# One retention head ahead of the four HGRN2 heads, and the last two modulation chunks computed in the downward stage

## The chip, the core and the metric

The kernel runs on one core of a Trainium2 chip. A core has a matrix engine (PE, with its weight loads listed apart as PEld), a vector engine (DVE), a scalar engine (ACT), a general engine (POOL) and sixteen DMA engines that are fed from queues; the queue of SP carries most transfers here and the queue of ACT the rest. Each engine works through its own list of instructions in order and waits on semaphores for the others. The metric is the device time of one execution in microseconds (us).

## The reference

One transformer block for 2048 rows of width 1024 and a context of 256 rows, all in float32. What matters here:

```python
mod_x = (silu(c) @ w_mod + b_mod)            # sh1, sc1, g1, sh2, sc2, g2, 1024 columns each
hx = rmsnorm(x, norm1_g) * (1 + sc1) + sh1   # 2048 rows; hc the same for the 256 context rows
p  = h @ w_in                                # hq, hi, hff, hfb, hg (HGRN2) and rq, rk, rv, rg (retention)
# HGRN2, 4 heads of 128: f = lb + (1 - lb) * sigmoid(z), forward and backward, k = 1 - f
#   scan in both directions with a decay per channel; rmsnorm((o_f + o_b) * sigmoid(hg))
# retention, 4 heads of 128: rotary embedding of rq and rk (x only), a fixed decay per head,
#   scan in both directions; rmsnorm(y_f + y_b) * silu(rg)
# both scans start from states that the context gives
x = x + g1 * (concat(8 heads) @ w_out)
h2 = rmsnorm(x, norm2_g) * (1 + sc2) + sh2
gate, up = split(h2 @ w_up)                  # 2 x 2816 columns
x = x + g2 * ((silu(conv3(gate)) * up) @ w_down)
return rmsnorm(x, final_g)
```

## The kernel before, in words

Matrices are multiplied in float16 pairs: each float32 operand is split into a high and a low part, and each product is three matmuls (`mm3`, lines 88 to 90). On top of that the products run as Winograd's form of Strassen's scheme: seven block products instead of eight, with sums of blocks made by DVE, ACT and POOL beforehand (`first_blocks` for the rows, `pair_blocks` for the weights) and sums of results afterwards (`unit`).

**Startup** (`setup`, `mod_first`, `heads`). The silu of c and c_ctx is multiplied by the columns of `w_mod` in chunks of 512; a chunk is called j4, and twelve chunks make the six vectors. Chunks 2, 3, 0 and 1 (scale and shift of the first norm) are multiplied on PE at the start, and the loads for it stand in SP's queue among those of the rows and of the first head's weights (`head_weights`, its loads and its preparation are items that are worked off one by one). `lower_bounds` makes the HGRN2 lower bounds with an exponential.

**Rows.** The 2048 rows are four groups g of 512. `norm_rows` and `first_blocks` turn a group into the seven block operands `hx` in float16 pairs. This takes DVE (lines 378, 387, 413, 416, 431), ACT (412, 433) and POOL (413, 451). Groups 3, 2, 1, 0 are made while the first head runs: `with_blocks` takes a step of the head's projection and a step of the next group's blocks by turns. The blocks are also written to DRAM (`hxd`), from where every later head reads them.

**Heads.** Eight heads run one after the other, HGRN2 0 to 3 and then retention 0 to 3. A head takes four steps, groups 3, 2, 1, 0. In a step, the head's backward sweep of one group (`hg_sweep1` or `ret_sweep1`) runs together with the forward sweep of a group of the head before (`sweep2`, `sweep2b`) and, as a filler, with the projection of the next group (`hg_proj`, `ret_proj`); `weave` says how many steps of the filler go between those of the sweep. The HGRN2 sweep goes through seven levels of doubling blocks, each with products on DVE (lines 874, 879, 759) that feed the next; the retention sweep has one decay mask and no levels. The context states come in a head's first step.

Alongside, `tick` works off a list: the next head's weights, and during the retention heads 0, 1 and 2 the chunks 4 to 6, 7 to 9 and 10 to 11 of the modulation (`mod_later`), which are eight DVE instructions of 128x512 each (lines 301, 303) and a few small matmuls (`mod_rows`, line 244). `ret_consts` makes the decay tables of the retention heads (lines 1102 to 1131) at the first step of the third head. The second half of the kernel is the output projection, the upward stage with its convolution and the downward stage (`ffn_down`), where seven block products, each for two halves of the rows, run from 2280 us to the end and `finish` writes the output. The gate g2 is spread over partitions into `gb` (`broadcast_cols`, line 1288) after the first of these; the first products with `gb` (line 1736) run in the second one, from 2347.5 us on.

**What sets the order.** The program is written once in this order; a planner then simulates it with costs of its own and lays down the order of the instructions on each engine. Buffers are rings named by tags ("Kl" has three, "gate" five, "wr" two), and an instruction waits until its ring has a free place.

Of the kernel before, what the change touches and what calls it, by code (L numbers as in the profile page):

```python
# [18 lines left out]
P = 128  # L19
# [24 lines left out]
SEQUENCE = 0, 1, 5, 6, 4, 3, 2  # L44

# [9 lines left out]
class Kern:  # L55
# [77 lines left out]
    def setup(self):  # L133
# [42 lines left out]
        self.W0, self.items0 = self.head_weights(0)  # L176
# [22 lines left out]
        self.smalls = s2, s1  # L199

# [32 lines left out]
    def mod_rows(self, rows, nr, j4):  # L233
# [12 lines left out]
        bm = view(self.sv, V_BM + 4 * j4, [[1, 4], [0, nr]])  # L246
        nc.vector.tensor_tensor(o, ps[:, :, :nr], bm, ALU.add)

    def mod_loads(self):
# [4 lines left out]
        for j4, places in ((2, ("hx",) * 4), (3, ("hx",) * 4), (0, KEPT[:4]), (1, ("FG", "KTt", "ou0", "ou1"))):  # L254
# [8 lines left out]
            if j4 in (3, 1):  # L263
                self.items0[0 if j4 == 3 else 4][0]()
# [14 lines left out]
    def mod_later(self, j4):  # L279
# [5 lines left out]
        def item(k0):  # L285
            def load():

                st[k0] = w = [self.slot_tile([P, 512], F32, "q", "wm") for _ in range(2)]
                for kk in range(2):
                    nc.sync.dma_start(w[kk], wsrc[:, k0 + kk, 512 * j4:512 * j4 + 512])  # L290

            def comp():
                if k0 == 0:
                    st["acc"] = self.slot_tile([P, 512], F32, "FG", "macc")
# [9 lines left out]
                if k0 + 2 == KT:  # L304
                    self.mod_rows(acc, 1, j4)
# [227 lines left out]
    def unit(self, mm, shape, banks, temps, evac, lin=(None, None), first=False):  # L533
# [5 lines left out]
        if first:  # L539
# [28 lines left out]
            add(tb, tb, u, ALU.add)  # L568
# [123 lines left out]
    def head_weights(self, h):  # L692
# [11 lines left out]
        for nm, tag, cols in want:  # L704
            raws, st = [], {}

            def load(cols=cols, raws=raws, tag="ou2" if h == 0 and nm == "q" else "wr"):
# [4 lines left out]
            def start(nm=nm, tag=tag, raws=raws, st=st):  # L712
# [7 lines left out]
                s, neg, dq = self.scales(self.allsum(ssq), self.dqx[:, 0:1] if h else None, "dq" + nm)  # L720
# [23 lines left out]
    def decay_gates(self, FG, X, h, n, W, first=False):  # L744
# [6 lines left out]
        yield from self.head_unit(*self.fm(w, X, n // 2), evac, first=first)  # L751
# [59 lines left out]
    def hg_proj(self, pool, h, g, W, pr, cur, first=False):  # L811
# [3 lines left out]
        yield from self.decay_gates(FG, X, h, G, W, first)  # L815
# [20 lines left out]
        yield from self.head_unit(*self.tm(w, X, H), evac, (dq, None), first)  # L836
# [125 lines left out]
    def hg_sweep2b(self, pool, h, g, st):  # L962
# [4 lines left out]
        m = r["qf"] if h < NH - 1 else pool.tile([P, G], F32, tag="Kl", bufs=KL, name="m")  # L967
# [14 lines left out]
    def step(self, h, i, W, cur, prev, pr):  # L982
# [3 lines left out]
        slot = i if h % 2 == 0 else NG - 1 - i  # L986
        hg, hgp = h < NH, h - 1 < NH
        if h < 2 * NH:
            main = (self.hg_sweep1 if hg else self.ret_sweep1)(pool, h % NH, g, slot, pr, cur)
        else:  # L990
            main = iter(())
        if prev is not None:
# [879 lines left out]
```

## Time and profile before

| | |
|---|---|
| median of 3 runs | 2695.32 us (2693.99 to 2698.18) |
| the profiled execution: its own time | 2692.15 us |
| its span, first to last instruction | 2690.3 us |
| mean granted clock of PE | 0.974 |
| busy in the span | PE 2532.6 us, DVE 1852.9, ACT 1335.7, POOL 776.8 |

How to read it: the span is counted from the first instruction; a stretch "46:309" is from 46 to 309 us after it. A row of a stretch gives for each engine its busy time and in brackets its instructions, then the clock that PE was granted as a part of full speed, the share of the DMA engines' time and the rate. A row of a group of instructions gives the line, engine and operation, out<-in, the count, and after the bar the busy time and the mean of one in ns; after the second bar stands how long the engine stood idle just before them and for whom. The head borders, read off the copies of each step's result: the first head's four steps end at 191, 229, 264 and 309 us, the three other HGRN2 heads at 476, 637 and 803 us, and the retention heads' sweeps end their last groups at 908, 1030, 1134 and 1234 us.

### The profile page before, as it was taken

How to read it: one execution, taken by the hardware profiler on the slowest of the kernel's cores; microseconds unless marked ns; L12 is line 12 of the kernel's file. 1: busy time of each engine (PE TensorE's matmuls, PEld its weight loads, DVE VectorE, ACT ScalarE, POOL GpSimd, SP SyncE). 2: the span in 40 equal slices, each digit the busy share in tenths (PEclk: the TensorE clock that was granted, in tenths of full speed). 3: DMA queues.
4: the chain of work that ended last, by engine and by line, in shares of the span. 5: the costliest groups of instructions: out<-in, count | busy, mean ns of one | idle time of the engine just before them, and what ended most of it. 6: DMA issues, size and time to landing. Idle time of an engine off the chain costs nothing.

```text
span 2690.3 us, 56082 instructions
## 1 busy us (share of the span) xinstructions
PE 2532.6 (94%) x22763; PEld 1669.3 (62%) x22763; DVE 1852.9 (69%) x3559; ACT 1335.7 (50%) x2846; POOL 776.8 (29%) x865
## 2 busy tenths in 40 slices
PE   5689999999999999998999899999999999999998
PEld 2578888888889889896444344444444444444443
DVE  4988667776767686767465878888888887323553
ACT  4766456664554444445455556555555555311210
POOL 3633112121123232221334344443443342000102
PEclk7899999999999999999999999999999999999999
DMA  7324234243337675756521223333323325634552
GB/s 262 145 84 158 87 119 147 73 154 118 104 130 254 194 249 185 250 182 198 198 98 48 94 91 118 102 110 114 118 98 106 116 92 203 247 131 187 203 196 94
DMA packets 213620, 393.97 MB, mean 146 GB/s; under 512 B 15599, under 2 KB 97747, under 8 KB 208752
## 3 DMA queue, kind: packets, MB, share of 16 engines
q1 hardware_dynamic: 203808, 373.42, 40.1%
q10 hardware_dynamic: 9248, 16.79, 1.9%
q8 instruction: 178, 2.92, 0.4%
q14 instruction: 82, 0.67, 0.1%
q0 software_dynamic: 304, 0.17, 0.0%
HBM read 298.57 MB, written 91.75 MB: 145 GB/s over the span
## 4 chain that ended last, share of the span: by engine, by line
PE 69%; DVE 16%; issue 5%; ACT 4%; DMA 3%; POOL 3%; SPq 0%; DVEq 0%; ACTq 0%; POOLq 0%
PE pa L88 7%; PE pa L89 7%; PE pa L90 7%; PE pd L88 5%; PE pd L90 5%; PE pd L89 5%; PE pc L88 3%; PE pc L89 3%; PE pc L90 3%; PE pb L88 2%; PE pb L89 2%; PE pb L90 2%; PE opp L88 2%; PE opp L89 2%; PE opp L90 2%
## 5 line engine op out<-in xcount | busy, mean ns | idle before, releaser
L88 PE MATMUL pa<-feat,w 128*128 128x512 f16 x704 | 264.5, 380 | 8.9 <-ACT ta L575 6.1
L89 PE MATMUL pa<-feat,w 128*128 128x512 f16 x704 | 267.5, 380 | 0.0
L90 PE MATMUL pa<-feat,w 128*128 128x512 f16 x704 | 266.9, 380 | 0.0
L89 PE MATMUL pd<-wd,actl 128*128 128x512 f16 x616 | 233.3, 379 | 0.0
L90 PE MATMUL pd<-wd,actl 128*128 128x512 f16 x616 | 233.3, 379 | 0.0
L88 PE MATMUL pd<-wd,actl 128*128 128x512 f16 x616 | 232.6, 379 | 0.0
L89 PEld LDWEIGHTS <-w 128*128 128x128 f16 x1232 | 120.6, 98 | 151.4 <-issue 13.2
L90 PEld LDWEIGHTS <-w 128*128 128x128 f16 x1232 | 120.8, 98 | 146.0 <-issue 1.7
L88 PEld LDWEIGHTS <-w 128*128 128x128 f16 x1232 | 120.7, 98 | 142.3 <-issue 2.6
L89 PEld LDWEIGHTS <-hx 128*128 128x128 f16 x1824 | 183.3, 100 | 7.4 <-issue 5.1
L88 PEld LDWEIGHTS <-hx 128*128 128x128 f16 x1824 | 183.5, 101 | 2.1
L90 PEld LDWEIGHTS <-hx 128*128 128x128 f16 x1824 | 182.8, 100 | 1.5 <-issue 0.7
L1622 ACT ACTIVATE st<-act,modT 128x512 f16<-128x512 f32 x154 | 107.3, 717 | 109.8 <-DVE act L1612 63.1
L1623 DVE SCALAR_TENSOR_TENSOR st<-act,modT,st 128x512 f16<-128x512 f32 x154 | 141.3, 953 | 29.6 <-ACT st L1622 28.9
L88 PE MATMUL pa<-w_vg,hx 128*128 128x128 f16 x800 | 145.2, 222 | 0.2
L90 PE MATMUL pa<-w_vg,hx 128*128 128x128 f16 x800 | 145.0, 222 | 0.0
L89 PE MATMUL pa<-w_vg,hx 128*128 128x128 f16 x800 | 144.9, 222 | 0.0
L88 PE MATMUL pc<-feat,w 128*128 128x512 f16 x352 | 134.0, 381 | 2.1 <-ACT feat L1397 1.1
L89 PE MATMUL pc<-feat,w 128*128 128x512 f16 x352 | 134.4, 382 | 0.1
L90 PE MATMUL pc<-feat,w 128*128 128x512 f16 x352 | 134.3, 382 | 0.0
L88 PE MATMUL pa<-hx,w_z 128*128 128x256 f16 x464 | 127.2, 274 | 5.5 <-DVE rV L617 4.1
L89 PEld LDWEIGHTS <-w_z 128*128 128x128 f16 x1072 | 107.3, 100 | 34.2 <-issue 23.7
(550 smaller groups left out, 7547.0 us busy)
## 6 DMA issues: line engine op xcount, KB each, us to landing
hx<-hxd SPq DMA_DIRECT2D x212, 512.0 KB, 4.6
actd<-st SPq DMA_DIRECT2D x154, 256.0 KB, 2.0
actl<-actd SPq DMA_DIRECT2D x28, 1024.0 KB, 5.0
wur<-in_w_up_dram SPq DMA_DIRECT2D x44, 512.0 KB, 3.8
raw<-in_w_in_dram SPq DMA_DIRECT2D x36, 512.0 KB, 4.4
wm<-in_w_mod_dram SPq DMA_DIRECT2D x64, 256.0 KB, 3.9
hxd<-hx SPq DMA_DIRECT2D x28, 512.0 KB, 3.6
wdb<-in_w_down_dram SPq DMA_DIRECT2D x44, 256.0 KB, 3.9
```

The source lines that it names most:

```text
L88: mm(ps, lhs(0), rhs(0), start=start, stop=False, skip_group_check=True)
L89: mm(ps, lhs(0), rhs(1), start=False, stop=False, skip_group_check=True)
L90: mm(ps, lhs(1), rhs(0), start=False, stop=stop, skip_group_check=True)
L1622: nc.scalar.activation(p[:, 0], v, AF.Copy, scale=s)
L1623: nc.vector.scalar_tensor_tensor(p[:, 1], v, s, p[:, 0], ALU.mult, ALU.subtract)
```

## The change

The heads run in the order retention 0, HGRN2 0 to 3, retention 1 to 3. So the rows' blocks are made beside a retention head. The tables of `ret_consts` are made in the startup, from loads on ACT's queue (`ret_loads`); `lower_bounds` moves into the first head's second step; the first head's weights are z and vg alone, without q; its rope tables come on SP's queue. Some temporaries lie in other buffers, and `with_blocks` spreads the blocks over 14 steps of the projection instead of 18. Chunks 10 and 11 of the modulation are taken out of retention head 2 and computed in the first three of the seven block products of the downward stage (`gates_later`), with `gb` behind them; the silu of c is kept in a place that lives that long (`keep`), and so is that part of the bias. Chunks 4 to 6 now go beside retention head 1 and 7 to 9 beside retention head 2. The output of a head goes through a tile of its own when the head behind is a retention head (`own`), and through `qf` otherwise.

```diff
+ORDER = 4, 0, 1, 2, 3, 5, 6, 7
...
-        self.W0, self.items0 = self.head_weights(0)
+        self.ret_loads()
+        self.W0, self.items0 = self.head_weights(ORDER[0], True)
...
         self.smalls = s2, s1
+        self.ret_consts()
...
     def mod_loads(self):
-            if j4 in (3, 1):
-                self.items0[0 if j4 == 3 else 4][0]()
+            if j4 == 3:
+                self.items0[0][0]()
...
-    def mod_later(self, j4):
+    def mod_later(self, j4, places=("q", "FG"), kept=False):
...
     def with_blocks(self, proj, blocks):
-        for j in range(18):
+        for j in range(14):
             next(proj)
-            if j in (5, 6, 7, 8, 9) or j > 11:
+            if 0 < j < 6 or j > 7:
                 next(blocks, None)
...
     def heads(self):
         self.mod_first()
-        items[5][0]()
         place = [self.gate_tile() for _ in range(4)]
         xc = self.load_rows(None, place)
         self.norm_rows(NG - 1, self.x3)
         for _, comp in items[:4]:
             comp()
-        self.lower_bounds()
+        items[4][0]()
...
-        first = self.hg_proj(pool, 0, NG - 1, W, pr, cur, True)
+        first = self.ret_proj(pool, ORDER[0] % NH, NG - 1, W, pr, cur, True)
...
-                    if NH <= h < 2 * NH - 1:
-                        mods = [it for c in ((4, 5, 6), (7, 8, 9), (10, 11))[h - NH] for it in self.mod_later(c)]
+                    if ORDER[p] in (5, 6):
+                        mods = [it for c in ((4, 5, 6), (7, 8, 9))[ORDER[p] - 5] for it in self.mod_later(c)]
...
-                blocks = self.first_blocks(0, rows(0, zq), self.temps(("ou2", "ou3", ("qf2", "qf3"), ("gate", "gate"))), "pj")
-            if s == 4 * 2:
-                self.ret_consts()
+                blocks = self.first_blocks(0, rows(0, zq), self.temps(("ou2", "ou3", "FG", ("gate", "gate"))), "pj")
+                self.lower_bounds()
...
+        keep = self.sv[:, V_LB + 6:V_LB + 14]
+        nc.vector.tensor_copy(keep, self.silc)
+        self.silc = keep
...
     def ret_proj(self, pool, h, g, W, pr, cur, first=False):
-            nc.scalar.dma_start(r, self.I["rope"][:, i, g * G:(g + 1) * G])
+            (nc.sync if first else nc.scalar).dma_start(r, self.I["rope"][:, i, g * G:(g + 1) * G])
...
+    def gates_later(self):
+        for j4 in (10, 11):
+            ahead = None
+            for load, comp in self.mod_later(j4, ("wr", "ou0"), True):
+                load()
+                yield
+                if ahead:
+                    ahead()
+                    yield
+                ahead = comp
+            ahead()
+            yield
+        dg = self.slot_tile([P, 2, P], F32, "xs", "diag")
+        self.broadcast_cols(lambda j: dg[:, j % 2], self.gb, 40)
+        yield
...
     def ffn_down(self):
+        late = self.gates_later()
...
                 self.work(1)
+                if n < 3:
+                    next(late, None)
             if m == 0 and t == 0:
-                dg = self.slot_tile([P, 2, P], F32, "xs", "diag")
-                self.broadcast_cols(lambda j: dg[:, j % 2], gb, 40)
                 fg = I["final_g"]
```

More of the change, by code (lines that the diff above doesn't have):

```diff
@@ L286, in load @@
             def load():
-                st[k0] = w = [self.slot_tile([P, 512], F32, "q", "wm") for _ in range(2)]
+                if places[0] == "wr":
+                    wr = self.slot_tile([P, 2, 512], F32, "wr", "wm")
+                    st[k0] = w = [wr[:, i] for i in range(2)]
+                else:
+                    st[k0] = w = [self.slot_tile([P, 512], F32, places[0], "wm") for _ in range(2)]
                 for kk in range(2):
@@ L705, in head_weights, with load @@
             raws, st = [], {}
-            def load(cols=cols, raws=raws, tag="ou2" if h == 0 and nm == "q" else "wr"):
+            def load(cols=cols, raws=raws, tag="wr"):
                 for c in cols:
@@ L814, in hg_proj @@
         FG = self.slot_tile([P, 2, G], F32, "FG", "FG")
-        yield from self.decay_gates(FG, X, h, G, W, first)
+        yield from self.decay_gates(FG, X, h, G, W)
         qs = pool.tile([P, G], F32, tag="qs", bufs=1, name="qs")
@@ L835, in evac @@
                 self.scaled(V[:, cs], c, s, dq)
[L836 removed]
+        yield from self.head_unit(*self.tm(w, X, H), evac, (dq, None))
         pr.update(FG=FG, K=K, Q=Q, qs=qs, ks=ks, V=V, gate=gate)
@@ L980, in weave, with step @@
             pass
-    def step(self, h, i, W, cur, prev, pr):
+    def step(self, p, i, W, cur, prev, pr):
         pool = self.mp
         g = NG - 1 - i
-        slot = i if h % 2 == 0 else NG - 1 - i
-        hg, hgp = h < NH, h - 1 < NH
-        if h < 2 * NH:
+        slot = i if p % 2 == 0 else NG - 1 - i
+        last = p == 2 * NH
+        h = None if last else ORDER[p]
+        hg = not last and h < NH
+        hp = ORDER[p - 1]
+        hgp = hp < NH
+        if not last:
             main = (self.hg_sweep1 if hg else self.ret_sweep1)(pool, h % NH, g, slot, pr, cur)
@@ L996, in step @@
             yield
-            if i == 0 and j == (1 if hg else 0) and h < 2 * NH:
+            if i == 0 and j == (1 if hg else 0) and not last:
                 yield from (self.hg_context if hg else self.ret_context)(pool, h % NH, W, cur)
-        if h or i:
+        if p or i:
             self.tick(self.n_tick)
         if prev is not None:
-            (self.hg_sweep2b if hgp else self.ret_sweep2b)(pool, (h - 1) % NH, i, prev)
+            sweep2b(pool, hp % NH, i, prev, not hg)
         yield from main
-        if h or i:
+        if p or i:
             self.tick(self.n_tick)
@@ L1212, in vg @@
                     self.scaled(V[:, cs], c, s, dqv)
-            yield from self.head_unit(*self.tm(w, X, H), vg, (dqv, None))
+            yield from self.head_unit(*self.tm(w, X, H), vg, (dqv, None), first)
             self.silu_bound(h, g, gate)
```

88 lines of the change are left out of this document (47 added, 41 removed).

## The prediction

> **What bounds the kernel now.** I read the page first, then busy time by stretches, then the chain of waits in the stretch that stands out.
>
> ```profile
> span 2690.3 us, 56082 instructions
> PE 2532.6 (94%) x22763; PEld 1669.3 (62%) x22763; DVE 1852.9 (69%) x3559; ACT 1335.7 (50%) x2846; POOL 776.8 (29%) x865
> ...
> DVE  4988667776767686767465878888888887323553
> PEclk7899999999999999999999999999999999999999
> PE 69%; DVE 16%; issue 5%; ACT 4%; DMA 3%; POOL 3%; SPq 0%; DVEq 0%; ACTq 0%; POOLq 0%
> ```
>
> PE is busy for 94% and carries 69% of the chain that ended last, so only PE's idle time, 158 us in all, and its slow clock can be won. Both sit at the left end: there DVE has its 9 and 8s and PEclk its only digits under 9. The stretches show how much lies there; the first head ends at 309 us, the HGRN2 heads at 803.
>
> ```profile
> core 0: us, PE busy (x) PEld busy (x) DVE busy (x) ACT busy (x) POOL busy (x), PEclk, DMA share, GB/s
> 46.00:85.00 39.00, 22.21 (x133) 16.26 (x133) 36.51 (x57) 28.03 (x55) 25.34 (x22) 0.63 0.42 155
> 104.00:229.00 125.00, 96.40 (x1404) 85.37 (x1403) 111.67 (x223) 84.79 (x201) 59.10 (x60) 0.88 0.28 107
> 46.00:229.00 183.00, 135.36 (x1770) 116.99 (x1771) 167.18 (x306) 128.22 (x287) 97.82 (x95) 0.84 0.34 125
> 46.00:309.00 263.00, 210.06 (x2960) 183.10 (x2961) 224.67 (x426) 172.24 (x382) 113.91 (x105) 0.87 0.37 129
> 309.00:803.00 494.00, 464.45 (x7640) 419.18 (x7638) 349.48 (x798) 273.00 (x685) 89.90 (x108) 0.98 0.35 117
> 816.00:936.00 120.00, 114.00 (x1382) 108.17 (x1382) 83.69 (x153) 55.85 (x142) 36.10 (x36) 0.99 0.67 221
> 1056.00:1166.00 110.00, 105.66 (x1255) 100.30 (x1254) 78.04 (x152) 48.68 (x126) 27.96 (x32) 0.98 0.65 218
> 816.00:1166.00 350.00, 332.31 (x3996) 315.42 (x3996) 245.79 (x460) 158.95 (x402) 98.94 (x104) 0.99 0.66 220
> 2275.00:2690.00 415.00, 406.08 (x1890) 185.24 (x1889) 175.61 (x265) 82.29 (x158) 34.19 (x116) 1.00 0.49 182
> ```
>
> From 46 to 229 us DVE is busy for 167.18 of 183 us (91%) and PE for 74%: here the rows are split into blocks beside the first head, and DVE sets the pace. From 309 to 803 us (three HGRN2 heads) PE is busy for 94%, from 816 to 1166 (three retention heads) for 95%: PE sets the pace, whatever the head. The chain of waits from 46 to 309 us, by line, says the same:
>
> ```profile
> by line: DVE ftmp L416 8.0%; DVE hx L413 7.3%; issue 5.1%; DVE Q L879 3.6%; PE p L88 3.3%; PE pa L88 3.1%; PE pa L89 3.1%; DVE ftmp L431 3.0%; PE p L89 2.9%; PE p L90 2.9%; PE pa L90 2.9%; DVE Q L822 2.8%; DVE junk L378 2.3%; DVE K L874 2.3
> ```
>
> Its largest pieces are DVE's block sums (416, 413), and the HGRN2 head's own products (879, 822, 874) stand in it with 8.7% of 263 us, 23 us.
>
> **The change part by part.** *The first head.* What the exchange takes off each engine comes from the two steady stretches, twelve steps each. DVE: 349.48/12 = 29.1 us in an HGRN2 step. A retention step has 245.79 us less the modulation chunks:
>
> ```profile
> L303 DVE SCALAR_TENSOR_TENSOR macc<-wm,silc,macc 128x512 f32<-128x512 f32 x56 | 47.4, 846 | 6.5 <-DMA wm<-in_w_mod_dram 5.9
> L1200 DVE TENSOR_TENSOR Q<-K,sin 64x1024 f32<-64x1024 f32 x12 | 18.8, 1566 | 9.4 <-ACT K L615 9.2
> L1222 DVE TENSOR_TENSOR K<-K,cos 128x1024 f32<-128x1024 f32 x13 | 17.7, 1365 | 0.0
> L301 DVE TENSOR_SCALAR macc<-wm,silc 128x512 f32<-128x512 f32 x8 | 4.6, 573 | 0.0
> ```
>
> (245.79 - 47.4 - 4.6)/12 = 16.1 us. The rotary products (1200, 1222 and its like) are in that. So 13.0 us per step go, 52 us over the head. PE: 464.45/12 - 332.31/12 = 38.7 - 27.7 = 11.0 per step, 44 us in all. What is left between 46 and 309 us is 172.7 us of DVE and 166 us of PE.
>
> How long does that take? At DVE's present share (224.67/263 = 85%) it is 202 us, 61 less; at PE's present share (80%) it is 208, 55 less. I take 60. By stretches: about 7 before 104 us, where q's weights and the gates' products go, 35 from 104 to 229, 18 after that, where PE leads. The bounds: at best DVE works at the 91% that it has up to 229 us, 172.7/0.91 = 190, 73 less; at worst only the HGRN2 pieces of the chain itself (23 us) and two thirds of the 18 go, 35 less.
>
> *Where the HGRN2 head lands.* It now costs what a steady one costs, 494/3 = 165 us. Out goes one of the three retention heads of 816 to 1166. Two stay: one as from 816 to 936 (120 us, twelve pairs of chunk instructions beside a head's weights) and one as from 1056 to 1166 (110 us), which now has 24 chunk instructions instead of 16. Eight more of 0.85 us make DVE 84.8 of 110 us, still under PE's 105.66; I charge half, 3.4. So 350 - 120 - 113.4 = 116.6 go and 165 come: **+48**. Bounds: 161 to 167 for the one (the three heads end at 476, 637 and 803 us), 110 to 120 for the other, so +41 to +57. The sweep of an HGRN2 group beside the forward sweep of a retention head has no row; its PE and DVE work is that of both, and POOL, through which the forward sweep's norm passes, is busy for 18% there.
>
> *The retention tables* leave the third head. Its first step stands beside the same step of the fourth:
>
> ```profile
> 476.00:529.00 53.00, 49.72 (x778) 45.11 (x776) 35.89 (x103) 28.71 (x71) 3.82 (x7) 1.00 0.23 76
> 637.00:690.00 53.00, 53.00 (x821) 48.63 (x820) 33.20 (x98) 24.70 (x64) 3.29 (x7) 1.00 0.22 77
> ```
>
> PE idles 3.3 us in the one and not at all in the other: **-3** (0 to -4). In the startup ACT has this hole for them:
>
> ```profile
> 15.64 0.63 ACT L376 ACTIVATE junk<-hc 128x512 f16<-128x512 f32 x1 [10.68 <-DMA hc<-in_x_dram]
> ...
> L1104 ACT ACT_TABLE_LOAD x1 | 1.3, 1283 | 0.0
> L1127 ACT ACTIVATE re<-ramp,tmp 128x128 f32<-128x128 f32 x8 | 2.8, 389 | 0.0
> ```
>
> Three table loads of 1.3 us, the eight exponentials of line 1127 and sixteen small ones come to about 11 us against 10.68 idle. The first squares (376) are next behind them on ACT, then the norm and the transposes, and PE's modulation matmuls queue behind those. I charge **+2** (0 to +6, half of the whole if the hole is missed). The ramp's load adds 256 KB to that time, and q's 512 KB go.
>
> *The lower bounds* leave this place:
>
> ```profile
> 37.73 1.28 ACT L226 ACT_TABLE_LOAD   x1
> ...
> 39.27 0.17 DVE L227 TENSOR_TENSOR tmp<-tmp 128x8 f32<-128x8 f32 x1 [2.31 <-ACT tmp L226]
> ```
>
> DVE waits 2.31 us here with the last shift (line 247) behind it, while nothing else runs: **-1** (0 to -2.3). In the second step two table loads come in, on an ACT that is busy for 68%: hidden.
>
> *Chunks 10 and 11.* Sixteen DVE instructions (13 us) and 4 MB go to the downward stage, where DVE is idle for 239 of 415 us and the DMA engines for half: hidden, without cover 13. PE is at 98% there, and the small matmuls (line 244) with their weights are in its queue with all products behind them. How they waited in the retention heads:
>
> ```profile
>   DVE macc L303: 8.1, 4
> ```
>
> PE's idle time for them was 8.1 us over 8 chunks, so two chunks cost 0 to 8 and on average 2; half of that is saved where they left: **+1**. SP's queue gets sixteen loads among those of the products; a place in "wr" is free a step ahead, so nothing stands behind them long. `gb` comes later than the first products with it did, and these move back into idle DVE time.
>
> **Sum:** -60 + 48 - 3 + 2 - 1 + 1 = **-13 us**. The profiled execution took 2692.15 us (1.85 outside its span), 3.2 under the median of the runs; so 2679 by its own time and **2682** by the median.
>
> [...] The row of the gates' product, in the first head and in the HGRN2 stretch after it:
>
> ```profile
> L822 DVE TENSOR_TENSOR Q<-qs,FG 128x512 f32<-128x512 f32 x10 | 10.2, 1045 | 0.1
> ...
> L822 DVE TENSOR_TENSOR Q<-qs,FG 128x512 f32<-128x512 f32 x22 | 15.6, 734 | 3.8 <-ACT qs L664 3.7
> ...
> L1199 POOL TENSOR_TENSOR Q<-K,sin x16: 2354/3334/3392, 769.1 to 1209.4; 64x1024 f32<-64x1024 f32 x16
> ```
>
> The same product takes 1045 ns where POOL is busy for 43% and 734 where it is for 18%. [...] The retention projection brings POOL's line 1199, 3.33 us four times, 13 us. [...]
>
> **The rivals.** *The block pipeline paces the first head (slower).* If the rows' blocks run ACT cast, POOL subtraction, DVE sum in a chain of their own, DVE's 91% is filler around it, and the HGRN2 products come out of gaps. Then only 35 us go: 2682 + 25 = **2707**. It decides from 47 us of saving down. For it: 416 and 413 lead the chain. Against it: DVE hardly idles, and whatever is taken off a full engine lets the next sum start.
>
> *The whole gain of DVE comes through.* At 91%, 73 us go: 2682 - 13 = **2669**. Against it: two steps follow PE, and those hold 80 of the 263 us.
>
> *The cover is thinner than it looks (no change).* Two forms. First, vg's weights:
>
> ```profile
> 79.25 0.27 PE L88 MATMUL pa<-hx,w_q 128*128 128x256 f16 x1
> 87.17 0.22 PE L88 MATMUL p<-w_vg,hx 128*128 128x128 f16 x1
> ...
> 92.93 0.74 DVE L675 SCALAR_TENSOR_TENSOR w_vg<-raw,p2s,w_vg 128x512 f16<-128x512 f32 x1
> ```
>
> Without q, PE wants vg at 79.25 instead of 87.17 us, and its last weights were split at 92.93: the 7 us before 104 go, **2689**. Second, PE's clock: it was 0.63 where PE was busy for 57%. With less PE work beside the same blocks it may stay there. From 104 to 229 us the work is 96.40 x 0.88 = 85 us at full clock, 22 less afterwards; 63/0.63 = 100 us where I count on 90: **2692**. [...]
>
> **How the numbers follow.** Forecast 2682 (2672 to 2690), chance 0.45; 2669, 0.2; no change, 2689 to 2696, 0.17; slower, 2707, 0.18. A measurement of this kernel tells 0.2% (5.4 us) from no change: under 2689.9 is faster, over 2700.7 slower. Faster: nine tenths of the first, the second whole, a third of the third: 0.66. Same: 0.17. Slower: 0.17. The range is 2658 to 2704: it leaves out a third of the second case and most of the last.
>
> **What would show it.** The first head's last result should be copied near 249 us instead of 309, DVE still near 85% to 91% busy until then; four HGRN2 heads of 161 to 167 us each, two retention heads of 120 and 113; no table loads in the third head; the modulation's last chunk of the startup no later than before; the downward stage as long as before (415 us from its first products to the end). I am wrong if the first head ends after 262 us (309 less 47), if an HGRN2 head beside retention takes 10 us more than its like, or if the downward stage grows by over 5.

## The result and the profile after

| | before | after |
|---|---|---|
| median of 15 runs each | 2695.32 us | 2701.70 us (2697.82 to 2707.73) |
| the profiled execution: its own time | 2692.15 us | 2705.32 us |
| its span | 2690.3 us | 2703.5 us |
| ratio | | 1.0031, 95% interval 1.0023 to 1.0038 |

The changed kernel is slower by 0.3%. The forecast was 2682 us, 0.5% faster, so the direction was wrong. The two profiled executions lie 13.2 us apart and the medians 6.4: the one of before is 3.2 us under its median, the one of after 3.6 over. Below, differences of traces are held against the 13.2 and differences of ratios against the 6.4.

The page of the changed kernel first: span, totals, the busy share of DVE and the clock granted to PE in 40 slices.

```profile
span 2703.5 us, 56062 instructions
PE 2536.1 (94%) x22763; PEld 1669.5 (62%) x22763; DVE 1857.1 (69%) x3554; ACT 1333.2 (49%) x2845; POOL 773.2 (29%) x860
...
DVE  5976586767758686676465878888888888333553
PEclk7799999999999999998999999999999999999999
```

The left end hardly looks better than it did: DVE still has its 9 and 7s there, and PEclk still has two digits under 9. The totals of PE and DVE agree within 0.3% with those of before; they tell nothing of the 13 us.

By stretches, the first three up to the end of the first head, one for the HGRN2 head behind it, one for the other three, and one for the steps of a retention head with chunks beside it (columns as in the prediction: length, then busy time of each engine, PE's clock, DMA):

```profile
46.00:131.00 85.00, 48.28 (x376) 39.68 (x377) 79.60 (x112) 55.71 (x118) 59.77 (x53) 0.68 0.44 155
131.00:210.00 79.00, 63.47 (x701) 56.83 (x701) 61.02 (x96) 54.59 (x122) 42.85 (x41) 0.93 0.34 123
210.00:271.00 61.00, 53.91 (x636) 49.97 (x635) 38.84 (x74) 32.62 (x71) 13.18 (x8) 0.95 0.51 174
46.00:271.00 225.00, 165.65 (x1709) 146.48 (x1710) 179.46 (x280) 142.92 (x309) 115.80 (x100) 0.84 0.42 149
271.00:436.00 165.00, 159.09 (x2596) 142.69 (x2594) 115.34 (x272) 86.90 (x216) 28.63 (x36) 0.99 0.38 123
436.00:925.00 489.00, 463.30 (x7642) 419.45 (x7641) 344.92 (x780) 259.97 (x653) 90.64 (x108) 0.99 0.36 118
938.00:1055.00 117.00, 111.91 (x1375) 106.16 (x1373) 83.09 (x152) 55.12 (x139) 36.18 (x36) 1.00 0.69 227
```

The kernel before, cut at the points that answer to the first three:

```profile
46.00:131.00 85.00, 51.30 (x508) 41.33 (x509) 80.46 (x126) 58.89 (x126) 59.38 (x57) 0.76 0.42 152
131.00:225.00 94.00, 80.06 (x1222) 72.02 (x1220) 83.65 (x170) 66.49 (x155) 38.44 (x38) 0.92 0.25 94
225.00:309.00 84.00, 78.69 (x1234) 69.75 (x1234) 60.56 (x133) 46.86 (x102) 16.09 (x10) 0.94 0.45 146
```

From 46 to 131 us nothing was won. At 131 us the rows of group 1 are normed in both kernels (130.85 before, 132.6 after), and DVE is busy for 95% and 94%. From there the blocks end after 79 us instead of 94, and the rest of the head takes 61 instead of 84. The DVE instructions that make the blocks (squares, scalings and sums, lines 385, 394, 420, 423, 438 and 442; before 378, 387, 413, 416, 431 and 435) cover the same number of elements in both kernels and take 100.9 us instead of 93.6. Of these 7.3 us, 5.5 fall before 131 us, where they eat up most of what the lighter head saves.

The borders of the heads are the copies of each step's result. Where the first head ends cannot be read off its own last copy (249.10 us, the time that the prediction named): a retention step copies early, 13 us after the step begins where a head follows an HGRN2 head (938.87 after 925.40 us). So I take the ends of the first and the fourth HGRN2 head. In after, and then in the kernel of the fourth experiment, whose instructions stand in the same order on PE, DVE and POOL until the last steps of the upward stage:

```profile
435.50 0.58 ACT L926 COPY ou<-op 128x512 f32<-128x512 f32 x1 [3.55 <-PE op L919]
925.40 0.59 ACT L926 COPY ou<-op 128x512 f32<-128x512 f32 x1 [2.91 <-PE op L919]
```

```profile
429.48 0.59 ACT L926 COPY ou<-op 128x512 f32<-128x512 f32 x1 [3.55 <-PE op L919]
925.07 0.59 ACT L926 COPY ou<-op 128x512 f32<-128x512 f32 x1 [2.91 <-PE op L919]
```

The same order of instructions gives 435.5 in one execution and 429.5 in another, and 925 in both. The kernel of the first experiment, whose order differs up to here by one small copy in the startup, gives 428.0 and 919.3; so a border in a single trace is good to some 6 to 8 us. With 165 us for the first HGRN2 head (an estimate: the three behind it take 163 to 165 us each in these executions, and PE is busy for 96% of 271 to 436 and for 95% of the stretch behind) the first retention head ends between 263 and 271 us. It saves 38 to 46 us where 60 were forecast. The last block is stored at 225.4 us before and at 207 to 210 in these three executions: up to there 16 to 19 us were saved, where the prediction has 42 (7 and 35), and behind it 22 to 27, where it has 18. Part by part, by the two profiled executions:

| part | before, us | after, us | measured | forecast |
|---|---|---|---|---|
| to the end of the last HGRN2 head | 802.9 | 925.4 | +122.5 | +103 |
| (of it to the scale of the rows, dqx) | 45.8 | 46.1 | (+0.3) | (+1) |
| the retention heads behind | 431.0 | 316.0 | -115.0 | -116.6 |
| to the last copy of a head | 49.0 | 48.0 | -1.0 | 0 |
| output projection and upward stage | 996.7 | 999.3 | +2.6 | 0 |
| downward stage | 410.7 | 414.8 | +4.1 | +1 |
| sum | | | +13.2 | -12.6 |

(+103 is -60 for the first head, +165 for the HGRN2 head that comes in, -3 for the tables and +1 for the startup.) Some 20 of the 26 us of the miss lie before 925 us and 3 in the downward stage; the 2.6 us of the output projection and the upward stage, which no edit touches, stay unexplained. By the medians the miss is 20 us and not 26; the rest is what the two profiled executions happened to take.

### The profile page after: what moved, and what is told of

Same layout as the page of the kernel before. It is cut to its first block, busy times and chain, and to the rows that moved or that the text cites. A ratio compares the mean times of both kernels' runs of the same rounds, so it can differ in the third digit from the quotient of the medians.

```text
span 2703.5 us, 56062 instructions
## 1 busy us (share of the span) xinstructions
PE 2536.1 (94%) x22763; PEld 1669.5 (62%) x22763; DVE 1857.1 (69%) x3554; ACT 1333.2 (49%) x2845; POOL 773.2 (29%) x860
## 4 chain that ended last, share of the span: by engine, by line
PE 48%; DVE 5%; DMA 2%; issue 1%; ACT 1%; POOL 0%; DVEq 0%; SPq 0%; POOLq 0%; ACTq 0%
PE pa L90 5%; PE pd L91 5%; PE pd L92 5%; PE pa L92 5%; PE pa L91 5%; PE pd L90 5%; PE pc L90 2%; PE pc L91 2%; PE pc L92 2%; PE opp L90 2%; PE opp L91 2%; PE opp L92 2%; PE pb L91 1%; PE pb L90 1%; PE pb L92 1%
## 5 line engine op out<-in xcount | busy, mean ns | idle before, releaser
L91 PEld LDWEIGHTS <-hx 128*128 128x128 f16 x1824 | 182.7, 100 | 10.4 <-issue 8.1
L90 PE MATMUL pa<-hx,w_z 128*128 128x256 f16 x464 | 127.8, 275 | 10.6 <-DVE ct L563 5.8
L91 PE MATMUL pa<-hx,w_z 128*128 128x256 f16 x464 | 127.9, 276 | 0.0
```

The costliest lines, as they stand in the source:

```text
L90: mm(ps, lhs(0), rhs(0), start=start, stop=False, skip_group_check=True)
L91: mm(ps, lhs(0), rhs(1), start=False, stop=False, skip_group_check=True)
```

## The experiments

Ratios are to the kernel before, timed on the same chip. One thousandth is 2.7 us. Where two ratios are compared, the interval of their difference is about 3 to 4 us each way. The runs were timed on five chips; the kernel after and the one with late chunks (the fourth experiment) were not timed again beside the runs that are held against them.

### The change in its three parts

**The order alone.** The gates stay in the heads; chunks 4 to 7 go beside retention head 1 and 8 to 11 beside retention head 2.

```diff
-mods = [it for c in ((4, 5, 6), (7, 8, 9))[ORDER[p] - 5] ...
+mods = [it for c in ((4, 5, 6, 7), (8, 9, 10, 11))[ORDER[p] - 5] ...
-        late = self.gates_later()
```

> The new order of the heads alone: chunks 10 and 11 of the modulation stay beside the retention heads (four chunks beside each of retention heads 1 and 2), gb is made after the first product of the downward stage as before. Theory A (the first head shrinks by only about 38 us instead of 60, and the downward stage pays for the chunks besides): the time stays above before, about 2698 us, ratio 1.001, since the downward stage gives back 5.5 us and the retention heads take 2 to 3. Theory B (the order is as good as forecast and the whole loss comes from the downward stage): about 2686 us, ratio 0.9965. In the trace both expect PE without a gap at the start of the downward stage.

Measured: 1.0072 (1.0057 to 1.0086), 11 us above after. The fourth HGRN2 head ends at 919.3 us, no later than in after, but the three retention heads take 337.5 us and not 316.0. The first of them and the sum of the three, here and then in after:

```profile
919.30:1037.40 118.10, 109.80 (x1302) 102.79 (x1300) 82.93 (x144) 53.55 (x136) 36.37 (x36) 0.97 0.71 237
...
sum 337.50, PE 309.75 PEld 291.39 DVE 232.17 ACT 148.64 POOL 85.61; mean PE 103.25 PEld 97.13 DVE 77.39 ACT 49.55 POOL 28.54
```

```profile
925.40:1028.70 103.30, 98.21 (x1216) 93.11 (x1214) 77.26 (x134) 52.21 (x133) 36.37 (x36) 1.00 0.75 245
...
sum 316.00, PE 297.22 PEld 281.55 DVE 222.84 ACT 147.72 POOL 84.11; mean PE 99.07 PEld 93.85 DVE 74.28 ACT 49.24 POOL 28.04
```

Two chunks more, 9.3 us of DVE, make these heads 21.5 us longer. PE's busy time grew by 12.5 us, for 1% more matmuls (3606 against 3570), at a lower clock (0.97 against 1.00 in the first head), and its idle time by 9. What of the clock is cause and what is consequence of the idle time, the run doesn't show. So taking the two chunks out of the heads was worth more in this order than I gave it, because only two heads are left to carry the chunks.

**The gates alone**, on the old order: chunks 10 and 11 in the downward stage, the rest as before.

```diff
-((4, 5, 6), (7, 8, 9), (10, 11))[h - NH]
+((4, 5, 6), (7, 8, 9), ())[h - NH]
+        late = self.gates_later()
```

> The old order of the heads, with chunks 10 and 11 and gb in the downward stage. Theory A: the loads and DVE products of chunk 10 are put ahead of the last transfers and weight splits that the downward stage waits for, PE idles 3 to 4 us at its start and has 2 us more of small matmuls, while retention head 2 gets 2 to 3 us shorter: about 2698 us, ratio 1.001. Theory B (the work is hidden, as forecast with +1): 2694 to 2696, ratio 0.9995 to 1.0005.

Measured: 1.0002 (0.9994 to 1.0011). The heads gain nothing (their last copy is at 1284.2 us, before at 1282.9), the downward products begin 4.9 us later than before, and they take 402.0 us instead of 400.0. PE waits 2 us for the first of them, as in after (the fourth experiment shows why). In the timed runs that is not told from no change.

**The tables alone**, on the old order: `ret_loads` and `ret_consts` in the startup.

```diff
+        self.ret_loads()
+        self.ret_consts()
-            if s == 4 * 2:
-                self.ret_consts()
```

> The old kernel with one thing moved: the tables of the retention heads are made in the startup instead of beside the third head. Theory A (PE idled for them in the third head, and ACT has the room in the startup): 4 us less, about 2691 us, ratio 0.9985. Theory B (the startup pays what the third head saves, or the gap in the third head had another cause): 2695, ratio 1.000.

Measured: 0.9995 (0.9987 to 1.0004). The HGRN2 heads end at 799.1 us instead of 802.9; at the last copy of a head, 1284.2 against 1282.9, it is gone. That the tables shorten the HGRN2 heads themselves is seen in more than this pair: from the end of the first to the end of the fourth, the three kernels that make them in the third head take 494.3 to 494.5 us, this one 488.2.

**After, with the gates' chunks begun with the second product** of the downward stage, two of their steps at a time.

```diff
-                if n < 3:
+                if 0 < n < 3:
+                    next(late, None)
                     next(late, None)
```

> The changed kernel, with chunks 10 and 11 begun with the second product of the downward stage instead of the first (two steps at a time). Theory A (the early loads and products delay the start of the stage): 3 to 4 us less than the changed kernel, about 2698 us, ratio 1.001, and no gap of PE before the first product. Theory B (the 11 us later start of the stage is all inherited from the heads): 2701 to 2702, ratio 1.0025.

Measured: 1.0008 (0.9999 to 1.0016), 6 us less than after. The seam to the downward stage shows why a part of it went. Before the first downward product, DVE has to scale the gain of the weights by a power of two (line 1742, before 1704), and ACT and DVE have to split the weights with it (1697, before 1676). In after:

```profile
2290.05 0.23 DVE L1742 TENSOR_SCALAR modT<-modT,p2s 128x11 f32<-128x11 f32 x1
2289.47 1.33 ACT L1643 ACTIVATE st<-act,modT 128x512 f16<-128x512 f32 x2 [6.08 <-issue]
2290.70 4.99 ACT L1697 ACTIVATE wd<-wdr,modT 128x512 f16<-128x512 f32 x8
2291.46 1.45 PE L90 MATMUL pd<-wd,actl 128*128 128x512 f16 x6 [1.99 <-ACT wd L1697]
```

Before, and then with the chunks begun late:

```profile
2279.16 0.22 DVE L1704 TENSOR_SCALAR modT<-modT,p2s 128x11 f32<-128x11 f32 x1
2279.42 5.01 ACT L1676 ACTIVATE wd<-wdr,modT 128x512 f16<-128x512 f32 x8 [3.94 <-DVE modT L1704]
```

```profile
2291.96 0.22 DVE L1742 TENSOR_SCALAR modT<-modT,p2s 128x11 f32<-128x11 f32 x1
2292.22 5.01 ACT L1697 ACTIVATE wd<-wdr,modT 128x512 f16<-128x512 f32 x8 [3.68 <-DVE modT L1742]
```

Before and with the late chunks the scale is there 0.4 and 0.7 us ahead of the last upward products (2279.6 and 2292.7 us), and the split follows at once. In after it comes 1.3 us behind them (2288.7), two splits of upward results (line 1643) stand ahead of the weights' on ACT, and PE waits 1.99 us. The loads of the gates do not hold the weights back: theirs is issued at 2261.28 us in after, 27 us ahead of the upward stage's end, as before (2255.11). What differs is the order that the planner laid down at the seam when it had the gates' steps to place there: in after the eight instructions of chunk 10 (lines 308 and 310, from 2271.0 us on) stand among DVE's last ones of the upward stage. The products still take 401.7 us and not 400.0; that is the time of the chunks' sixteen small matmuls (line 248, 1.9 us), which have no cover on a PE that is busy throughout (in after for 401.61 us of the 401.70 from 2292.0 us on).

The traces give the late chunks 2.4 us and not 6: from the last upward product to the end the stage takes 412.4 us in each of the six kernels that have them, and 414.8 to 416.3 in the nine whose chunks begin early, after among them. The other 4 us have no place in the stage. So the 1.0008 of this kernel may be low by that much, and the runs below that start from it, all between 1.0012 and 1.0025, may be held against too good a figure.

### What sets the pace of the first head

The theory of the prediction was that DVE does, since it is busy for 91% of the time in which the blocks are made. The runs take work off one engine, move it to another, or change its order. Those that start from after are compared with 1.0031, those with the late gates with 1.0008 (with 1.0022, if the late chunks are worth the 2.4 us of the traces).

**No rotary products** in the three groups that run beside the blocks.

```diff
-        nc.gpsimd.tensor_tensor(pt[64:], qk[:64], sines[:64], ALU.mult)
+        if not first:
+            nc.gpsimd.tensor_tensor(pt[64:], qk[:64], sines[:64], ALU.mult)
...
```

> Left out: the rotary products of the first head in the three groups that run beside the rows' blocks (lines 1219, 1220, 1242, 1243); their keys and queries stay as projected. DVE loses 3 x (1.8 + 1.5 + 1.4) = 14 us there, POOL 3 x 2.46 = 7.4. The time goes by the kernel after, 2701.7. Theory D (VectorE sets the pace of the first head; it is busy for 86% from 46 to 210 us): 14/0.86 = 16 us less, 2686, and the first HGRN2 head ends near 415 to 420 us instead of 430 to 435. Theory C (a chain sets it: rows' norm on POOL, transposes, blocks, the next rows into the freed places, their norm; VectorE's other work lies in its gaps): 4 us less at most, 2698 to 2702.

Measured: 0.9972 (0.9961 to 0.9983), 16 us less, and the first HGRN2 head ends at 418.5 us. As the theory of DVE has it.

**POOL's half of the rotary products on DVE.**

```diff
-        nc.gpsimd.tensor_tensor(pt[64:], ...)
+        (nc.vector if first else nc.gpsimd).tensor_tensor(pt[64:], ...)
```

> POOL's half of the rotary products (line 1219) goes to VectorE in the same three groups; nothing is left out. VectorE gets 3 x 1.8 = 5.4 us more, POOL loses 7.4. Theory D: 5.4/0.86 = 6 us more, 2708. Theory P (what holds VectorE up is POOL beside it: a block sum takes 1010 ns here and 811 in the kernel before): VectorE's other instructions get back 3 to 5 us, so 2700 to 2703. Theory C: within 2 us, 2700 to 2704.

Measured: 1.0027 (1.0015 to 1.0040), 1 us less than after where DVE's work alone asked for 6 more. DVE took the 5.4 us, and the rows below give back 5.1. These are its block sums (line 423), the rows' scaling (394) and the sums that read PSUM (438) from 46 to 210 us; first in after, then in this kernel, then before, where the lines are 416, 387 and 431:

```profile
L423 DVE TENSOR_TENSOR ftmp<-ftmp 128x512 f32<-128x512 f32 x21 | 24.5, 1169 | 1.1 <-POOL hx L420 1.0
L438 DVE TENSOR_SCALAR ftmp<-tp,A,B 128x512 f32<-128x512 f32 x15 | 12.1, 805 | 11.2 <-PE tp L401 11.2
L394 DVE TENSOR_SCALAR gate<-gate,rs_y 128x512 f32<-128x512 f32 x2 | 3.9, 1969 | 0.0
```

```profile
L423 DVE TENSOR_TENSOR ftmp<-ftmp 128x512 f32<-128x512 f32 x21 | 20.7, 992 | 0.3 <-POOL hx L420 0.2
L438 DVE TENSOR_SCALAR ftmp<-tp,A,B 128x512 f32<-128x512 f32 x15 | 12.0, 804 | 3.5 <-PE tp L401 3.5
L394 DVE TENSOR_SCALAR gate<-gate,rs_y 128x512 f32<-128x512 f32 x2 | 2.7, 1382 | 0.0
```

```profile
L416 DVE TENSOR_TENSOR ftmp<-ftmp 128x512 f32<-128x512 f32 x16 | 14.5, 918 | 0.0
L431 DVE TENSOR_SCALAR ftmp<-tp,A,B 128x512 f32<-128x512 f32 x15 | 12.0, 802 | 0.0
L387 DVE TENSOR_SCALAR gate<-gate,rs_y 128x512 f32<-128x512 f32 x2 | 0.9, 480 | 0.0
```

The block sum took 918 ns before, 1169 after, and 992 with POOL's products gone; the scaling of the context's rows went from 480 to 1969. The sums that read PSUM took 802 to 805 in all three. One place in after shows how (start, length):

```profile
98.76 3.86 DVE L394 TENSOR_SCALAR gate<-gate,rs_y 128x512 f32<-128x512 f32 x2
98.58 1.27 POOL L458 TENSOR_TENSOR ftmp<-ftmp 128x512 f32<-128x512 f32 x1 [1.35 <-DVE ftmp L423]
99.93 2.40 POOL L1219 TENSOR_TENSOR Q<-K,sin 64x1024 f32<-64x1024 f32 x1
```

Two scalings that take 0.48 us each in the kernel before, from 92.14 us on, where POOL is idle beside them (91.57 to 94.85 us), fill 98.76 to 102.62 here: 1.38 us over a POOL sum of 1.27 us, and 2.56 over its product of 2.40. So the busy time of DVE holds 0.90 and 2.08 us in these two places that the same instruction does not take with POOL idle. What the slow ones have in common is not shown: the block sums (918 to 1169 ns) have two tensors as input, the scaling (480 to 1969 ns) one, and no run isolates one pair of instructions.

**The rows' inverse norms on DVE** instead of POOL, for the context and groups 1 and 0, by a shift and three Newton steps.

```diff
-        r = self.rstd(self.mp, ssq[:, :nt], nt, D)
+        r = self.rstd_v(ssq[:, :nt], nt, D) if g in (None, 1, 0) else self.rstd(...)
```

> The rows' inverse norms of the context and of the groups 1 and 0 are worked out by twelve small VectorE instructions of 0.16 us (shift, subtraction, three Newton steps) instead of six on POOL, where they took 7 us (125.5 to 132.5 and 164.1 to 170.7). Nothing is left out. Theory C: the transposes of group 1 and of group 0 start 4 to 5 us earlier each, so 8 to 10 us in all, 2692 to 2694, and the last block of group 0 is stored near 201 instead of 210. Theory D: 3 x 2 us more of VectorE, 2702 to 2708.

Measured: 1.0038 (1.0025 to 1.0052), no gain; the last block is stored at 211.5 us, not 201. But the norms got no shorter: their small instructions stood in DVE's queue between others, and from the sum of the squares to the scaling group 1 took 10.4 us (117.9 to 128.3; in after 7.3) and group 0 took 7.8 (166.8 to 174.7; in after 6.8). So the run shows that moving them doesn't help, and not what a shorter norm would bring.

**A quarter of the head's products**, so that PE is light: `nk` is 1 in the three groups and 4 elsewhere.

```diff
-            for k in range(4):
+            for k in range(nk):
```

> Left out: three quarters of the contraction of the first head's products in the same three groups (one of four blocks of 128 rows is multiplied), 1.5 x 28 us of TensorE at full clock, 41 us; what evacuates and splits stays. Theory T (TensorE's queue and its clock of 0.80 hold up the transposes): the three groups take 20 to 40 us less, 2662 to 2682. Theories D and C: the waits for transposes (11.2 us from 46 to 210) fall by some 8, the rest stays, because VectorE or the norms pace it: 2690 to 2696.

Measured: 0.9966 (0.9955 to 0.9978), 17.5 us less, between the two forecasts. From 46 to 206 us in after, without rotary products, and with light products:

```profile
46.00:206.00 160.00, 108.90 (x1062) 94.66 (x1063) 136.73 (x203) 107.99 (x234) 98.70 (x89) 0.81 0.40 142
```

```profile
46.00:206.00 160.00, 118.59 (x1215) 104.73 (x1216) 131.14 (x211) 117.46 (x256) 91.78 (x91) 0.84 0.47 165
```

```profile
46.00:206.00 160.00, 86.09 (x629) 69.30 (x630) 147.30 (x215) 114.52 (x252) 105.79 (x93) 0.70 0.44 160
```

With PE light, DVE is busy for 147.30 of 160 us; with less on DVE, PE is, for 118.59 instead of 108.90. Both runs store the last block at 196 us instead of 210 (`hxd`, here in after, without rotary products and with light products):

```profile
L422 SPq DMA_DIRECT2D hxd<-hx x28: 319/320/1093, 60.2 to 209.6; - x28
```

```profile
L422 SPq DMA_DIRECT2D hxd<-hx x28: 319/320/385, 60.0 to 195.9; - x28
```

```profile
L422 SPq DMA_DIRECT2D hxd<-hx x28: 319/320/699, 59.2 to 196.3; - x28
```

Neither engine alone holds the head back.

**The blocks' place in the order.** Four runs, all with the late gates: the projection and its blocks twice as fast against the sweep, or at 0.7 of the speed (2 and 0.7 in the first diff); a block piece behind each of the first nine pieces of a projection; and the squares of rows on ScalarE.

```diff
+            if blocks:
+                n_fill *= 2
```

> The kernel with the gates' chunks begun late (which stood at 1.0008 of before), and in the first head's first two steps the projection with the blocks of the next rows is advanced twice as fast against the sweep. Nothing is left out. Theory W (the shorter sweep lets the head run ahead of the blocks: the first group's partial output is copied at 135 us, 190 before, while the rows of group 1 are normed at 132 as before; so the removed VectorE work was not what stood ahead of the blocks): the blocks end 5 to 10 us earlier than the 206 to 210 of after and the time falls by 5 to 8 us, to 0.998. Theory D (VectorE's whole work counts, in whatever order): within 3 us of 1.0008.

> The same with the projection and the blocks advanced at 0.7 of their speed against the sweep. Theory W: the blocks end 5 to 10 us later, the time rises by 4 to 8 us, to 1.003. Theory D: within 3 us of 1.0008.

```diff
-            if 0 < j < 6 or j > 7:
+            if j < 9:
```

> The late gates again, and each of the first nine pieces of a projection is followed by one piece of the blocks (before: pieces 1 to 5 and from 8 on), so the transposes stand two products further ahead in TensorE's queue. Nothing is left out. Theory W: 2 to 5 us less, 0.9995. Theory D: within 3 us of 1.0008.

```diff
-                if g == NG - 1 or h or g in (None, 0):
+                if True:
```

> The late gates again, and the eight squares of rows that VectorE takes (line 385, in the groups 2 and 1) go to ScalarE, which takes the others and is busy for 67% from 46 to 210 us. Nothing is left out. VectorE loses 8 x 0.8 = 6.5 us. Theory D, by the rate of the run without rotary products (16 us of time for 14 of VectorE): 7 us less, 0.998. Theory W or any chain through the norms: the norms wait for ScalarE's squares behind its casts, and the time stays or rises by up to 3 us, 1.0008 to 1.002.

Measured: 1.0013 (1.0002 to 1.0025), 1.0017 (1.0008 to 1.0026), 1.0022 (1.0012 to 1.0031) and 1.0012 (1.0002 to 1.0021), against 1.0008 with none of this. None of the orders gains anything that can be told. But none of the first three brought the blocks to an earlier end either: the last one is stored at 211.7, 210.5 and 214.1 us, with late gates alone at 206.7. So they don't show what blocks that end earlier would bring. The fourth speaks against DVE; the kernel with late gates, and then this one:

```profile
46.00:206.00 160.00, 107.28 (x1070) 93.12 (x1071) 139.24 (x204) 109.29 (x237) 100.97 (x92) 0.83 0.40 142
```

```profile
46.00:206.00 160.00, 110.66 (x1064) 94.98 (x1065) 131.84 (x188) 111.69 (x250) 98.72 (x89) 0.81 0.39 142
```

DVE has 131.84 us there where the kernel with late gates has 139.24, and nothing is gained against 1.0008 (against 1.0022 it would be 2.7 us, less than can be told). ScalarE took the squares over: 111.69 against 109.29 us in this stretch and 61.95 against 56.78 before 131 us.

**Work or wait?** The rotary products made, but into the scratch tile in the first head's three groups, so that the scores don't wait for them.

```diff
+        o = pt if first else qk
...
-            nc.vector.tensor_tensor(qk, qk, view(cos, ...), ALU.mult)
-        nc.vector.tensor_tensor(qk, qk, pt, ALU.add)
+            nc.vector.tensor_tensor(o, qk, view(cos, ...), ALU.mult)
+        nc.vector.tensor_tensor(o, o, pt, ALU.add)
```

> The kernel after, where in the three groups beside the blocks the rotary products are all computed, by the same engines on tiles of the same size, but written to the scratch tile: the scores take the unrotated keys and queries and wait for none of it. Left out: the rotation in those groups' scores. Theory D (VectorE's work counts): as after, 1.003. Theory H (each step's chain counts: projection, rotary products, scores; 1.4 + 1.3 + what stands ahead of them on VectorE): most of the 16 us of the run without rotary products, to 0.998 or 0.997.

Measured: 1.0026 (1.0016 to 1.0037), 1 us less than after. The wait costs nothing that can be told; the work does. In the real kernel with late gates, the same two products ahead of the second projection:

```diff
+        if first:
+            nc.vector.tensor_tensor(qk, qk, view(cos, ...), ALU.mult)
+            nc.vector.tensor_tensor(qk, qk, pt, ALU.add)
         V = pool.tile(...)
```

> The kernel with the gates' chunks begun late (1.0008 of before), and in the three groups the cosine product and the sum (lines 1242, 1243) are issued right behind the sine products, ahead of the second projection, instead of behind its last evacuation. Nothing is left out. Theory H: the scores no longer wait for them, 3 us a group, 8 us in all, 0.998. Theory D: the same work, within 2 us of 1.0008.

Measured: 1.0025 (1.0015 to 1.0034), against 1.0008: no gain, rather 4 us of loss, of which most goes if the figure to hold it against is 1.0022. Theory H falls twice.

**Both cuts at once**: neither rotary products nor the full contraction.

> Both the rotary products and three quarters of the contraction left out in those three groups. Alone they brought 16 and 17.5 us. Theory H (the time is the sum of the waits along the order in which four queues are filled): they add up to nearly 33 us, 0.991. Theory F (the blocks have a floor of their own, some 196 us for their last store, which both runs reached): 20 us, 0.9955.

Measured: 0.9932 (0.9919 to 0.9945), 26.7 us less than after. The two gains add up in part (33 would be all), and there is no floor at 20.

**The squares in the kernel before** on ScalarE, with the edit of the twelfth run.

> The kernel before, with the eight squares of rows that VectorE takes in the groups 2 and 1 (line 378) on ScalarE. Nothing is left out. VectorE, busy for 91% from 46 to 229 us, loses 6.5 us there. Theory D of the prediction (VectorE sets the pace of the first head): 6 to 7 us less, 0.9975. Theory H: within 2 us of 1.000; the 91% is then no sign of what sets the pace.

Measured: 0.9991 (0.9982 to 1.0000), 2.4 us less where DVE's pace asked for 6 to 7. So DVE's 91% alone did not set the pace in the kernel before either; what ScalarE's added work took back of the 6.5 us is not told apart here.

**No squares on DVE and none elsewhere**, in after.

```diff
+                if not h and g in (1, 2):
+                    continue
```

> The kernel after without the eight squares of rows that VectorE takes in the groups 2 and 1 (line 385, 8.2 us at 1031 ns). Left out: half of the columns in those groups' norms; the other half's sum is counted twice. Theory A (work taken off any of the engines counts, work moved to another does not: rotary products left out -16 us, moved to VectorE 0, squares moved to ScalarE 0): 6 to 9 us less than after, 1.000. Theory R (only the rotary products count, through their place between projection and scores; squares lie in gaps): within 2 us of after, 1.003.

Measured: 1.0016 (1.0006 to 1.0026), 4 us less than after, between the two theories.

Taken together: work moved between DVE, POOL and ACT changed 2.4 us at most (four runs); a wait taken away or an order changed brought no gain (five runs, two of them some 4 us slower by their ratios); work taken away brought 0.4 to 0.75 us for each us (17.5 of 41 on PE, 4 of 8.2 on DVE, 16 of 21.4 on DVE and POOL, 26.7 of 62 for both cuts). The change itself took 45.2 us off DVE and 44.4 off PE up to the end of the first head (224.67 to 179.46 and 210.06 to 165.65) and won 38 to 46, which is 0.4 to 0.5 for each us of the two. That is near the same rate, but it was found after the fact, and ACT's 29.3 us less (172.24 to 142.92) are not in it; with them it is 0.3 to 0.4. It is a summary and not a rule to forecast by. Why the rate is what it is, that is, which hand-overs between the four queues make it up, the runs don't settle.

**A kernel faster than both.** The kernel before with the tables in the startup and DVE's squares on ScalarE, no other change.

> The kernel before with the two edits that stood lowest alone: the retention tables in the startup (0.9995) and VectorE's eight squares on ScalarE (0.9991). Nothing is left out. If they add up 0.9986; if the first head takes the one back as it did with the tables, 0.9992 to 0.9997.

Measured: 0.9980 (0.9971 to 0.9989), 5.4 us less than before. Its HGRN2 heads end at 793.5 us, before at 802.9.

## Why the prediction was wrong

**Where it failed: "At DVE's present share (224.67/263 = 85%) it is 202 us ... I take 60."** The step took the engine with the highest share for the one that sets the pace, and let its work and the time shrink together, and PE's with it. Two things broke it. First, DVE's work shrank by 45 us and not by 52, because the instructions that make the blocks took 100.9 us instead of 93.6. That they stand beside POOL, whose 115.80 us now lie in 225 and not in 263 us, fits this, and the run with POOL's products moved away supports it (992 ns for a block sum instead of 1169). Second, the shares did not hold: DVE fell from 85% to 80% and PE from 80% to 74% of the shorter time. Each engine had less to do and waited more for the others. What remains for DVE, 179.46 us, at the old 85% would have been 210 us; the head took 225 (217 and 218 in the two other executions). So 8 us of the miss are work that grew, and 7 to 15 are shares that fell. By stretches the step failed where the blocks are made: 42 us were forecast up to their end and 16 to 19 came, while behind it, where the prediction has PE in the lead, 22 to 27 came for 18. That DVE's share alone does not set the time is shown; what sets it in its place, beyond work on several engines that counts in part, stays open.

**The bounds held, but barely.** "At worst" was 35 us, and 38 to 46 came; near the end that I gave little weight, since I held that "whatever is taken off a full engine lets the next sum start". The run that moved squares from DVE to ScalarE in the kernel before speaks against that: 6.5 us went off the engine and 2.4 off the time.

**The rival that came nearest** was the block pipeline, 2707 us. Its sign is there: the first head ends after 262 us, and less than 47 us went. Its mechanism is neither shown nor ruled out: the rotary wait, taken away, brought nothing, and TensorE's work, which has no place in it, counted; but no run made the norms shorter or brought the blocks to an earlier end by order alone.

**POOL's rotary products** were seen coming, 3.33 us four times, beside a row of DVE that took 1045 ns where POOL is busy for 43% and 734 where it is for 18%, and I charged nothing for them, because I took that slowing to be in the steady rows of DVE's rotary product already. What POOL's products do to the block sums and scalings (992 ns for a block sum without them, 1169 with them) was not in those rows. Their size was off as well: beside the blocks POOL's product took 2.4 to 2.6 us and not 3.33 (7.4 us for the three groups).

**Where the HGRN2 head lands**: +48 forecast; 163 to 165 in, by the three others, and 115.0 out against 116.6. Right as far as the traces tell; the first of the four is not measured by itself. That the chunks beside only two heads are dear was not seen (the order alone, 1.0072), and the change avoided it.

**The tables**: -3 forecast; by the traces -5 in these heads (494.5 to 489.9, though the other execution with the same order has 495.6), one table load of seven is left there, that of the gate's silu (line 1230), and alone the tables change the time by -1.3 us, with an interval from -3.5 to +1.1. **The startup**: +0.3 against +1, right; ACT's hole held the tables.

**Chunks 10 and 11**: +1 forecast. Their DVE work and their loads are hidden, as I said; the small matmuls cost the 2 us that I named as PE's part. What I had left out is the seam: I looked at places in the ring and in SP's queue, and not at the order of the last steps of the stage before, which cost another 2 us. The stage grew by 4.1 us, under the 5 that I set as the sign; 6 us went when the chunks began later, of which the traces show 2.4.

**The chances**: 0.17 for slower was too little for a sum whose largest term hung on one reading of a busy share, and the measured time is inside the range (2658 to 2704).

## What to carry to other kernels

A share of 91% on one engine was no proof here that it sets the pace, with four queues that feed each other (6.5 us moved off it brought 2.4): before counting on it, move one small piece of its work elsewhere and see whether the time follows. Where DVE and POOL worked side by side here, instructions of DVE were busy for longer (a scaling of 480 ns for 1380 and 2558), and work moved between the two was worth nothing that could be told in two runs, while work taken away counted with 0.4 to 0.75 of its length. When work is moved into a stage, let it begin behind that stage's first products, so that it cannot disturb the order at the seam (2.4 us here). And check in the trace that an experiment moved what it was meant to move: here a norm that was given to another engine took as long as before.

## What the hardware showed that I had not expected

- The same DVE instruction, a 128x512 scaling of rows, took 480 ns with POOL idle beside it, 1380 ns over a POOL sum of 1.27 us and 2558 ns over a POOL product of 2.40 us; the sums that read PSUM took 802 to 805 ns on average in the three kernels where they were compared.
- Two executions of the same order of instructions differed by 6 us at 430 us of the trace and by 0.3 us at 925, and a third with almost that order by 7.5 and 6.1: a difference that appears in one place of two profiles need not be one of the kernels.
- With two chunks more beside the retention heads PE's busy time grew by 4% for 1% more matmuls, while its granted clock went from 1.00 to 0.97 in the first of them and PE's idle time there from 5.1 to 8.3 us. Which of the two brings the other about, no run here isolates.
